# Preparing the first latent head's keys and queries ahead of four gate projections

## The chip, the cores and the metric

The kernel runs on one core of a Trainium2 chip. The metric is device time in microseconds (us) for one execution of the whole program. The core has a matrix engine (PE, with its weight loads PEld), a vector engine (DVE), an activation engine (ACT), a general engine (POOL) and the engine SP, whose queue issues nearly all the transfers of this kernel. Matrix results land in PSUM banks, from which ACT and DVE copy them to SBUF.

## The reference, cut to what matters

Two layers of a streaming encoder, for a prompt of 512 rows and a sample group of 64 rows with 1024 cached rows. Layer 0 runs latent attention (A) and stick-breaking attention (B) side by side; layer 1 runs two other attentions. Each layer ends in a gated output projection. What the change touches is attention A of the prompt group:

```
q_a, kv_a, k_r, g_a, ... = split_cols(h @ w_in, EVEN_SIZES)
c_kv   = rmsnorm(kv_a, kv_norm)            # latent, 128 wide
k_rope = apply_rope(k_r, pos)              # 32 wide
q      = einsum('bsc,chr->bshr', rmsnorm(q_a, q_norm), w_uq)   # 8 heads of 64 + 32
s      = (q . [w_uk c_kv ; k_rope]) * A_SCALE      # masked, then softmax per head
out_a  = (softmax(s) @ c_kv) @ w_uv
mixed  = [silu(g_a) * out_a ; silu(g_b) * out_b];  x += rmsnorm(mixed @ w_out)
```

The kernel builds the per-head keys (64 rows from `w_uk`, 32 rotary rows) and splits most operands in a high and a low part, so that most products are three matmuls.

## The kernel before, in words

The stretch in question is the passage from attention B to attention A in layer 0. In program order it reads:

1. `mla_queries(0)` (L968 on) projects the queries of heads 0 to 3, rotates them (`rope_q`) and leaves them in four tiles `qs`; `mla_vals(0)` makes the values of heads 0 to 3.
2. The last pair of heads of attention B, `sb_pair(3)`, with its sample part beside it, inside `tc.high_priority(PR_last)`.
3. Four gate projections, `gate_tile(a["ws"][12 + p], ...)`: each has two halves of weights (loaded, split by ACT into a high part `whi` at L166 and by POOL into a low part `wlo` at L170), two PSUM banks of 24 matmuls each (`ws_bank`, L253), and per bank one sigmoid on ACT (L624) and one product on DVE (L625).
4. The key tiles of head 0: `KH0`, `KL0` (high and low part) and the split of `w_uk` into `wukh`, `wukl` (L1016 to L1025); the rotary key rows are transposed on PE (L1023) and copied by ACT (L1024) and DVE (L1025).
5. Loads of `wuv` and `wukT` (L1027, L1028); the cached keys and values of the sample group (L1075 to L1106), most of them into the tile `arena`, which takes the room of `h0`'s first half and so waits for the last gate matmul that reads it.
6. `mix0`: four gated outputs of attention B are copied and split into the operand of the output projection (`mix`, high part on ACT L655, low part in turn on POOL and DVE, L656). It takes the room of `h0`'s second half.
7. `mla_prep(0)` (L932 on): three matmuls for head 0's keys (L939), evacuated by ACT (L940) and DVE (L941) into `KH0`, `KL0`; four transposes for its queries (L945), evacuated by ACT (L946) and DVE (L947) into two tiles `QH`, `QL`.
8. `mla_squeries(0)`, `mla_vals(1)` (L909 matmuls, L913 on ACT, L914 on DVE), and then the heads: `mla_head` prepares head h+1 and computes the scores of head h (L963, L964), whose first step on DVE is the row minimum L919.

What sets the order: the program runs in a planner that goes through the instructions, takes for each engine the one that comes first in program order among those that it holds ready by its own costs, and gives out the buffers as it goes; each engine then executes its list strictly in order. `high_priority` moves a block forward in that preference. So program order is a preference between instructions that are ready and no fixed place.

Buffers that the change touches: PSUM tag `psA` has two banks, shared by `gate_tile`, `mla_queries`, `mla_vals`, `mla_prep` and others; `psT` has two banks for transposes. The ring `R` has ten SBUF tiles: four for each pair of attention B, `wvh`, `wvl`, the four of step 4, `wuv`, `wukT`, and two per prepared head. `wraw` has four buffers for weights as loaded; `whi` and `wlo` have five each.

Of the kernel before, what the change touches and what calls it, by code (L numbers as in the profile page):

```python
# [26 lines left out]
NPAIR = H // 2  # L27
# [32 lines left out]
def f32(ap):  # L60
    return ap.bitcast(F32)
# [3 lines left out]
def kernel(ctx: ExitStack, tc: tile.TileContext, a: dict, o: dict):  # L65
# [11 lines left out]
    def nm(s):  # L77
        cnt[0] += 1
        return f"{s}_{cnt[0]}"
# [14 lines left out]
    def ring(shape, dt, tag, name=None):  # L94
        p, n = rings[tag]
        if isinstance(p, list):
            rings[tag][1] += 1
            return p[n % len(p)].tile(shape, dt, name=nm(name or tag), tag=tag, bufs=1)
        return p.tile(shape, dt, name=nm(name or tag), tag=tag, bufs=n)
# [4 lines left out]
    def Er(shape, name="e"):  # L104
        return ring(shape, F32, "E", name)

    def Rr(shape, name="r"):
        return ring(shape, F32R, "R", name)
# [49 lines left out]
    phase = [""]  # L158
# [80 lines left out]
    def ws_tiles(h, tiles, between=None):  # L239

        ws = [ws_weights(src, rooms) for src, _, rooms in tiles]
        for c0, c1 in CUTS:
            for (_, cb, _), w in zip(tiles, ws):
                ws_bank(w, h, cb, c0, c1)
            if between and c1 < TT:
                between()
# [56 lines left out]
    def drain():  # L303
        for _ in side[0]:
            pass
# [308 lines left out]
    def gate_tile(src, h, ft, raw):  # L614
        g = bp.tile([P, TT], F32, name=nm("g"), tag=f"g{ft}", bufs=1)
        gates[ft] = g

        def cb(ps, c0, c1):
            n = c1 - c0
            gv = g[:, c0:c1]  # L620
            th = Er([P, 320], "th")
            tv = th[:, :n]
            if raw:
                nc.scalar.activation(tv, ps[:, :n], AF.Sigmoid)  # L624
                nc.vector.tensor_mul(gv, ps[:, :n], tv)  # L625
            else:

                nc.scalar.activation(tv, ps[:, :n], AF.Tanh, scale=0.5)
                nc.vector.scalar_tensor_tensor(out=gv, in0=tv, scalar=1.0, in1=ps[:, :n], op0=ALU.add, op1=ALU.mult)

        ws_tiles(h, ((src, cb, ()),))
# [14 lines left out]
    def new_h(pool):  # L646
        f = new_feat(pool)
        for g in range(2):
            feat_half(f, g, g)
        return f  # L650
# [111 lines left out]
    h0 = new_h(big)  # L762
# [170 lines left out]
    def mla_prep(h):  # L933

        st = h % 2
        kp = psA()
        hs = slice(h * 64, (h + 1) * 64)
        for n, (w, c) in enumerate(((wukh, CTh), (wukh, CTl), (wukl, CTh))):
            nc.tensor.matmul(kp[:64], w[:, hs], c[:, 2, :S], start=(n == 0), stop=(n == 2))  # L939
        nc.scalar.copy(KH[st][:64], kp[:64])  # L940
        nc.vector.tensor_sub(KL[st][:64], kp[:64], f32(KH[st][:64]))  # L941
        QH, QL = Rr([P, S]), Rr([P, S])
        tp = psA()
        for t in range(NT):
            nc.tensor.transpose(tp[:96, t * P:(t + 1) * P], qt[h // 4][t][:, h % 4, :], ident)  # L945
        nc.scalar.copy(QH[:96], tp[:96])  # L946
        nc.vector.tensor_sub(QL[:96], tp[:96], f32(QH[:96]))  # L947
        return QH, QL
# [59 lines left out]
    with tc.high_priority(PR_last):  # L1008
        beside(sb_sample(3), EV_sb)
        sb_pair(3, pr)  # L1010
        drain()
    for p in range(NPAIR):
        gate_tile(a["ws"][12 + p], h0, p, True)

    phase[0] = ""
    KH0, KL0, wukh, wukl = (Rr([P, 512], x) for x in ("kh0", "kl0", "wukh", "wukl"))  # L1016
    wkr = w_tile("wraw", [P, 512], F32)
    nc.sync.dma_start(wkr, a["w_uk"])
# [4 lines left out]
        nc.tensor.transpose(tp[:32, t * P:(t + 1) * P], kr[:, t], ident)  # L1023
    nc.scalar.copy(KH0[64:96], tp[:32])  # L1024
    nc.vector.tensor_sub(KL0[64:96], tp[:32], f32(KH0[64:96]))  # L1025
    wuv, wukT = ring([P, 512], F32, "R", "wuv"), ring([P, NPAIR, P], F32, "R", "wukT")
    nc.sync.dma_start(wuv, a["w_uv"])  # L1027
    nc.sync.dma_start(wukT, a["w_ukT"])  # L1028
# [15 lines left out]
    def mla_squeries(hh):  # L1044

        qn = ring([P, 4, 64], F32, "sx", "qn")
        nc.gpsimd.tensor_copy(out=qn[:DS], in_=qf[:, 4 * hh:4 * hh + 4, :64])
        qnf = qn.rearrange("p h d -> p (h d)")
        t = psT()
        for p in range(2):  # L1050
            nc.tensor.transpose(t[:, p * DS:(p + 1) * DS], qnf[:DS, p * P:(p + 1) * P], ident[:DS, :DS])
        qnT = ring([P, P], F32, "sx", "qnT")
        nc.scalar.copy(qnT, t[:, :P])
        for s in range(2):
            t = psT()
            me = slice(64 * s, 64 * s + 64)
            for p in range(2):
                nc.tensor.matmul(t[:, p * DS:(p + 1) * DS], wukT[me, 2 * hh + p, :], qnT[me, p * DS:(p + 1) * DS],
                                 start=True, stop=True)
            tv = v3(t[:, :P])  # L1060
            qh, ql = (x[:, hh * 256:(hh + 1) * 256].rearrange("p (a s b) -> p a s b", a=2, s=2)[:, :, s, :]
                      for x in (QLh, QLl))
            nc.scalar.copy(qh, tv)
            nc.vector.tensor_sub(ql, tv, f32(qh))
        qh4 = qf[:, 4 * hh:4 * hh + 4, 64:96]
        qr3 = ring([P, 4, 96], F32R, "sx", "qr3")
        nc.scalar.copy(qr3[:DS, :, 0:32], qh4)
        nc.scalar.copy(qr3[:DS, :, 64:96], qh4)
        nc.vector.tensor_sub(qr3[:DS, :, 32:64], qh4, f32(qr3[:DS, :, 0:32]))
        t = psT()  # L1070
        for h in range(4):
            nc.tensor.transpose(t[:96, h * DS:(h + 1) * DS], f32(qr3)[:DS, h, :], ident[:DS, :DS])
        nc.scalar.copy(QR[:96, hh * 256:(hh + 1) * 256], t[:96, :256])
# [64 lines left out]
    for p in range(NPAIR):  # L1138
        mix(mix0, 1, p, gates[4 + p], eng=nc.vector if p % 2 else nc.gpsimd)
        mix_sample(mix0, 1, p, gates[4 + p])  # L1140
    QLh, QLl, KH1, KL1 = (bp.tile([P, 512], F32R, name=x, tag=f"g{i}", bufs=1)
                          for i, x in ((4, "qlh"), (5, "qll"), (6, "kh1"), (7, "kl1")))
    KH, KL = (KH0, KH1), (KL0, KL1)
    for x in (KH, KL):
        nc.gpsimd.tensor_copy(out=x[1][64:96], in_=f32(x[0][64:96]))
    part0 = dp.tile([TT, D], F32, name="part0")
    ready = {0: mla_prep(0)}
    mla_squeries(0)
    mla_vals(1)
    def mla_samples():  # L1150
# [365 lines left out]
def build(arrays):  # L1516
    import concourse.bacc as bacc

    nc = bacc.Bacc("TRN2", target_bir_lowering=False, num_devices=1)
    a, o = {}, {}  # L1520
    for name, v in arrays.items():
        a[name] = nc.dram_tensor(f"in_{name}_dram", v.shape, mybir.dt.from_np(v.dtype), kind="ExternalInput").ap()
    for i, (name, shape) in enumerate(_OUTS):
        ap = nc.dram_tensor(f"out_{i}_dram", shape, F32, kind="ExternalOutput").ap()
        rows = [d for d in shape if d != 1][0]
        n = int(np.prod(shape)) // rows
        o[name] = bass.AP(ap.tensor, 0, [[n, rows], [1, n]])
    with tile.TileContext(nc, schedule_with_timeline_sim=True) as tc:
        kernel(tc, a, o)
    return nc  # L1530
# [9 lines left out]
```

## Time and profile before

| what | value |
|---|---|
| median of 3 runs | 844.62 us (844.27 to 845.49) |
| profiled execution, its own time | 845.28 us |
| span in the trace, first to last instruction | 842.8 us |
| PE busy | 773.1 us (92% of the span) |
| DVE busy | 596.8 us (71%) |
| ACT busy | 451.0 us (54%) |
| POOL busy | 364.5 us (43%) |
| mean granted clock of PE | 0.978 of full speed |

The profiled execution takes 2.5 us more than its span and 0.66 us more than the median. A row of the timeline gives start, duration, engine, line, operation and operands, with the idle time of the engine before it and what ended that in brackets. All times of rows are us from the start of the span.

### The profile page before, as it was taken

To read this page: it belongs to the slowest core of one execution; us is meant where nothing else is said; L and a number is where in the kernel's file an instruction comes from. 1 tells how busy PE (TensorE), PEld (TensorE's weight loads), DVE (VectorE), ACT (ScalarE), POOL (GpSimd) and SP (SyncE) were. 2 spreads that over 40 slices of the span, in tenths; PEclk is the share of its full clock that TensorE was granted. 3 is DMA by queue.
4 is the path that set the end of the run, shared out by engine and by line. 5 is a ranking of instruction groups with operands and counts; after the bars stand their busy time and mean duration, and the time that the engine had idled before them with its cause. 6 is when DMAs were issued, how large, how long until landed. Compare 5 with 4: busy or idle time off the path is not lost.

```text
span 842.8 us, 16341 instructions
## 1 busy us (share of the span) xinstructions
PE 773.1 (92%) x5581; PEld 716.0 (85%) x5581; DVE 596.8 (71%) x1453; ACT 451.0 (54%) x1232; POOL 364.5 (43%) x464
## 2 busy tenths in 40 slices
PE   8889899999896999998889999999998999999996
PEld 6889798988795788796788989999997898998986
DVE  5566887797956767658984766686766777778655
ACT  7533563565755666554553545465434665658521
POOL 6574343554527012125673444353234343436343
PEclk9999999999998999998999999999999999999999
DMA  8143323622121111236353443334234442452472
GB/s 250 58 126 116 93 77 96 194 79 94 57 85 48 61 53 60 82 96 238 113 143 113 137 123 102 112 101 119 71 108 115 155 143 83 136 155 68 139 236 100
DMA packets 69924, 95.52 MB, mean 113 GB/s; under 512 B 9529, under 2 KB 40489, under 8 KB 69810
## 3 DMA queue, kind: packets, MB, share of 16 engines
q1 hardware_dynamic: 69264, 94.12, 36.8%
q8 instruction: 44, 0.72, 0.3%
q10 hardware_dynamic: 578, 0.37, 0.1%
q14 instruction: 38, 0.31, 0.1%
HBM read 74.36 MB, written 18.79 MB: 111 GB/s over the span
## 4 chain that ended last, share of the span: by engine, by line
PE 60%; DVE 16%; ACT 6%; issue 6%; DMA 5%; POOL 5%; SPq 1%; DVEq 0%; POOLq 0%; ACTq 0%
PE psA L253 21%; PE psA L263 15%; PE psU L427 4%; PE psX L516 4%; PE psT L418 3%; PE psA L271 3%; DVE r L361 2%; POOL wlo L170 2%; DVE whi L168 1%; PE psS L452 1%; DVE C L477 1%; PE psS L551 1%; DMA wraw<-in_w_out_dram 1%; PE psS L453 1%; ACT sx L570 1%
## 5 line engine op out<-in xcount | busy, mean ns | idle before, releaser
L253 PE MATMUL psA<-hT,whi 128*128 128x320 f32 (+1 forms) x1216 | 259.0, 301 | 5.4 <-DVE r L341 2.0
L170 POOL TENSOR_TENSOR wlo<-wraw,whi 128x512 fp32r<-128x512 f32 (+2 forms) x102 | 138.9, 1368 | 184.8 <-ACT whi L166 97.1
L253 PEld LDWEIGHTS psA<-hT,whi 128*128 128x128 f32 x1216 | 199.6, 191 | 8.8 <-DVE g L625 1.7
L253 PE MATMUL psA<-hT,wlo 128*128 128x320 f32 (+1 forms) x608 | 183.3, 302 | 0.0
L263 PE MATMUL psA<-whi,hT 128*128 128x256 f32 (+2 forms) x812 | 163.1, 288 | 8.3 <-DVE m L733 6.5
L263 PEld LDWEIGHTS psA<-whi,hT 128*128 128x128 f32 x812 | 130.2, 189 | 11.8 <-DVE m L733 7.7
L263 PE MATMUL psA<-wlo,hT 128*128 128x256 f32 (+2 forms) x420 | 121.4, 289 | 0.0
L253 PEld LDWEIGHTS psA<-hT,wlo 128*128 128x128 f32 x608 | 116.0, 191 | 0.3
L263 PEld LDWEIGHTS psA<-wlo,hT 128*128 128x128 f32 x420 | 80.1, 191 | 0.5
L166 ACT CAST whi<-wraw 128x512 fp32r<-128x512 f32 (+2 forms) x72 | 43.9, 614 | 33.7 <-PE psA L253 25.4
L168 DVE CAST whi<-wraw 128x512 fp32r<-128x512 f32 (+1 forms) x58 | 39.0, 674 | 18.9 <-PE psA L263 8.0
L363 POOL TENSOR_TENSOR kz<-kf,r 64x256 fp32r<-64x256 f32 x48 | 40.8, 851 | 23.3 <-DVE r L361 20.9
L477 DVE TENSOR_TENSOR_SCAN C<-C 128x384 f32<-128x384 f32 (+4 forms) x44 | 46.3, 1062 | 6.4 <-ACT C L475 6.1
L461 ACT ACTIVATE x<-x,st 128x128 f32<-128x128 f32 (+1 forms) x64 | 36.0, 562 | 22.2 <-DVE st L1227 21.7
L422 DVE TENSOR_TENSOR pt1l<-psT,pt1h 128x384 fp32r<-128x384 f32 x64 | 39.5, 619 | 10.2 <-ACT pt1h L421 9.1
L516 PE MATMUL psX<-vs,sP 128*128 128x256 f32 (+1 forms) x184 | 40.5, 315 | 6.4 <-DVE vs L543 5.6
L529 POOL TENSOR_TENSOR sK<-kraw,sK 128x384 fp32r<-128x384 f32 (+2 forms) x32 | 32.5, 1016 | 30.4 <-ACT sK L528 24.6
L421 ACT CAST pt1h<-psT 128x384 fp32r<-128x384 f32 x64 | 34.0, 533 | 21.7 <-PE psT L418 20.2
L439 POOL TENSOR_TENSOR g<-g,oT 128x512 f32<-128x512 f32 x14 | 18.9, 1347 | 56.5 <-DVE oT L431 56.4
L452 PE MATMUL psS<-r,r 128*128 128x256 f32 (+1 forms) x96 | 34.6, 362 | 6.7 <-DVE st L1227 6.2
L1227 DVE CUSTOM_DVE_ANT_0 x<-psS,T 128x128 f32<-128x128 f32 (+1 forms) x64 | 30.8, 481 | 11.4 <-PE psT L418 10.1
L431 DVE SCALAR_TENSOR_TENSOR oT<-psU,oT 64x256 f32<-64x256 f32 x64 | 26.8, 419 | 16.9 <-ACT oT L430 15.9
(391 smaller groups left out, 1953.0 us busy)
## 6 DMA issues: line engine op xcount, KB each, us to landing
wraw<-in_ws_dram SPq DMA_DIRECT2D x80, 256.0 KB, 2.8
wraw<-in_w_out_dram SPq DMA_DIRECT2D x32, 256.0 KB, 2.8
x<-in_x_prompt_dram SPq DMA_DIRECT2D x16, 256.0 KB, 5.2
part<-part SPq DMA_DIRECT2D x32, 128.0 KB, 2.1
m<-part SPq DMA_DIRECT2D x16, 256.0 KB, 5.6
r<-r SPq DMA_DIRECT2D x48, 64.0 KB, 2.0
out_dram<-kout SPq DMA_DIRECT2D x12, 256.0 KB, 2.7
out_dram<-vf SPq DMA_DIRECT2D x24, 128.0 KB, 1.8
```

Source lines behind the costliest of these rows:

```text
L166: nc.scalar.copy(hi, raw)
L168: nc.vector.tensor_copy(out=hi, in_=raw)
L170: eng.tensor_sub(lo, raw, f32(hi))
L253: nc.tensor.matmul(ps[:, :c1 - c0], w[:, k % 4, :], h.m[k // 4][:, k % 4, x, c0:c1], start=(k == 0 and n == 0), stop=(k == KT - 1 and n == 2))
L263: nc.tensor.matmul(ps[:, :n], h.m[k // 4][:, k % 4, x, t * P:(t + 1) * P], w[:, k % kp, :], start=(k == ks[0] and m == 0), stop=(k == ks[- ...
L363: nc.gpsimd.tensor_sub(pair.kl[s][me, cs], kf[me, cs], f32(k[me, cs]))
L421: nc.scalar.copy(ph[:, :i + 1, at], tv)
L422: nc.vector.tensor_sub(pl[:, :i + 1, at], tv, f32(ph[:, :i + 1, at]))
L452: nc.tensor.matmul(ps[:, :w], pair.qq[s][:, q], pair.kk[s][:, :w], start=True, stop=False)
L461: nc.scalar.activation(w[:, :n], src, AF.Exp, bias=mn, scale=-1.0, accum_out=sm)
L477: nc.vector.tensor_tensor_scan(out=c[:, :n][:, ::-1], data0=c[:, :n][:, ::-1], data1=c[:, :n][:, ::-1], initial=1.0 if carry is None else ...
L516: nc.tensor.matmul(po[:, :256], l, r, start=(first and n == 0), stop=(last and n == len(ops) - 1))
```

## The change

`mla_prep(0)` and the key tiles it needs (steps 4 and 7) are put ahead of the four gate projections (step 3). The pair lists `KH`, `KL` are made early with only their first entry; the second, `KH1`, `KL1`, is filled in where it was made before. The three matmuls, four transposes, their four copies, the load and split of `w_uk`, and the rotary key rows all stay the same instructions; the loads of `wuv` and `wukT` stay behind the gates. The assignment `phase[0] = ""` (which engines split weights) stays behind the gates as well.

```
         sb_pair(3, pr)
         drain()
-    for p in range(NPAIR):
-        gate_tile(a["ws"][12 + p], h0, p, True)
-
-    phase[0] = ""
+
     KH0, KL0, wukh, wukl = (Rr([P, 512], x) for x in ("kh0", "kl0", "wukh", "wukl"))
     wkr = w_tile("wraw", [P, 512], F32)
     nc.sync.dma_start(wkr, a["w_uk"])
...
     nc.vector.tensor_sub(KL0[64:96], tp[:32], f32(KH0[64:96]))
+    KH, KL = [KH0, None], [KL0, None]
+    ready = {0: mla_prep(0)}
+    for p in range(NPAIR):
+        gate_tile(a["ws"][12 + p], h0, p, True)
+
+    phase[0] = ""
     wuv, wukT = ring([P, 512], F32, "R", "wuv"), ring([P, NPAIR, P], F32, "R", "wukT")
...
-    KH, KL = (KH0, KH1), (KL0, KL1)
+    KH[1], KL[1] = KH1, KL1
     for x in (KH, KL):
         nc.gpsimd.tensor_copy(out=x[1][64:96], in_=f32(x[0][64:96]))
     part0 = dp.tile([TT, D], F32, name="part0")
-    ready = {0: mla_prep(0)}
     mla_squeries(0)
     mla_vals(1)
```

## Rows read from the trace of the kernel before

**Rows 1.** Busy time by stretch: length, PE, PEld, DVE, ACT, POOL, PE clock, DMA.
```profile
219.50:228.50 9.00, 6.21 (x43) 4.68 (x41) 8.97 (x17) 7.37 (x20) 7.20 (x9) 1.00 0.23 81
228.50:260.40 31.90, 31.90 (x243) 31.05 (x242) 17.44 (x35) 16.06 (x38) 7.83 (x12) 1.00 0.20 63
260.40:270.30 9.90, 2.79 (x19) 1.52 (x17) 8.20 (x8) 5.16 (x14) 9.76 (x9) 0.79 0.33 93
270.30:276.40 6.10, 6.08 (x25) 5.40 (x26) 4.75 (x12) 3.90 (x9) 3.97 (x4) 0.51 0.46 136
276.40:400.00 123.60, 115.59 (x800) 100.30 (x799) 85.95 (x250) 74.21 (x211) 28.68 (x34) 0.97 0.30 94
...
```
**Rows 2.** What PE waited for from 260 to 345 us: total, times, longest.
```profile
PE psA L909 <- DVE kl L941: 5.2, 1, 5.2
PE psS L963 <- ACT r L946: 1.4, 1, 1.4
...
```
**Rows 3.** Timeline of PE, 256 to 275 us, six of its rows.
```profile
256.00 0.60 PE L1023 MATMUL psT<-ident,kr 128*32 128x128 f32 x4
...
260.61 0.66 PE L1058 MATMUL psT<-qnT,wukT 64*128 64x64 f32 x8
261.73 0.44 PE L939 MATMUL psA<-cth,wukh 128*64 128x512 f32 x1 [0.46 <-ACT ks L1089]
...
262.24 0.39 PE L939 MATMUL psA<-cth,wukl 128*64 128x512 f32 x1
262.71 0.64 PE L945 MATMUL psA<-ident,qs 128*96 128x128 f32 x4
...
274.28 0.63 PE L909 MATMUL psA<-r,cth 128*128 128x256 f32 x2
```
**Rows 4.** Timeline of DVE, 264 to 274 us, six of its rows.
```profile
264.82 3.45 DVE L656 TENSOR_TENSOR hT<-g,hT 128x512 fp32r<-128x512 f32 x2
268.19 1.48 DVE L168 CAST whi<-wraw 128x512 fp32r<-128x512 f32 x1
269.60 0.67 DVE L941 TENSOR_TENSOR kl<-psA,kh 64x512 fp32r<-64x512 f32 x1
270.20 0.67 DVE L947 TENSOR_TENSOR r<-psA,r 96x512 fp32r<-96x512 f32 x1
270.79 1.50 DVE L170 TENSOR_TENSOR wlo<-wraw,whi 128x512 fp32r<-128x512 f32 x1
...
272.95 0.27 DVE L919 TENSOR_REDUCE st<-psS 128x1 f32<-128x128 f32 x1
...
```
**Rows 5.** Timeline of ACT, 261 to 265 us, one row.
```profile
263.65 0.58 ACT L940 CAST kh<-psA 64x512 fp32r<-64x512 f32 x1
...
```
**Rows 6.** All L168 copies of the kernel: duration in ns, least, median, most.
```profile
L168 DVE CAST whi<-wraw x58: 390/428/1549, 40.0 to 806.6; 128x512 fp32r<-128x512 f32 x56, 128x528 fp32r<-128x528 f32 x2
```
**Rows 7.** Busy time by stretch, columns as in rows 1, one stretch of 2 us.
```profile
266.00:268.00 2.00, 0.00 (x0) 0.00 (x0) 2.00 (x2) 0.79 (x3) 2.00 (x3) 0.52 0.23 83
...
```
**Rows 8.** Timeline of PE, DVE and POOL around the first gate matmul, one fence.
```profile
227.85 1.33 POOL L1020 TENSOR_TENSOR wukl<-wraw,wukh 128x512 fp32r<-128x512 f32 x1 [0.73 <-ACT wukh L1019]
228.02 0.39 DVE L914 TENSOR_TENSOR v<-psA,v 128x256 fp32r<-128x256 f32 x1
228.46 0.51 PE L253 MATMUL psA<-hT,whi 128*128 128x256 f32 x2
229.97 0.41 DVE L914 TENSOR_TENSOR v<-psA,v 128x256 fp32r<-128x256 f32 x1
233.42 0.39 DVE L625 TENSOR_TENSOR g<-psA,th 128x256 f32<-128x256 f32 x1
...
```
**Rows 9.** Timeline of SP and POOL, loads and the last step of `sb_pair(3)`.
```profile
224.57 0.33 SPq L1018 DMA_DIRECT2D wraw<-in_w_uk_dram  x1
249.79 0.43 SPq L1028 DMA_DIRECT2D wukT<-in_w_ukT_dram  x1
254.11 1.29 POOL L439 TENSOR_TENSOR g<-g,oT 128x512 f32<-128x512 f32 x1 [9.02 <-DVE oT L431]
```

## The prediction

> **What bounds the kernel now.** The page comes first: PE is busy for 92% of the span, so time is lost where PE stands still or runs slowly. The busy table by stretch around the moved step shows where [rows 1]. From 219.5 to 228.5 us DVE is full (8.97 of 9.00 us) and PE stands still for 9.00 - 6.21 = 2.8 us. From 228.5 to 260.4 PE is full: that is the four gate projections with the rest of `sb_pair(3)` between them. From 260.4 to 270.3 PE works 2.79 of 9.90 us while POOL is full (9.76) and DVE nearly (8.20). From 270.3 to 276.4 PE is full again, but its granted clock is 0.51. From there to 400 us PE is busy for 115.59 of 123.60 us.
>
> The list of waits names the hole: 5.2 us of PE, once, for DVE's L941, and 1.4 us for ACT's L946 [rows 2]. Both are evacuations of `mla_prep(0)`. In PE's timeline its seven matrix instructions (three L939, four L945) stand at 261.7 to 263.4, right behind the gates, and the third of the four L909 groups of `mla_vals(1)` starts only at 274.28 [rows 3]. ACT makes its key copy at 263.65, at once [rows 5]. DVE comes to the matching L941 at 269.60, because two subtractions of `mix0` (L656, 3.45 us) and a weight copy (L168) stand ahead of it in its list; L947 follows, then a weight subtraction (L170), and the first softmax step of head 0, L919, starts at 272.95 [rows 4]. Both banks of `psA` are held until L941 and L947 are done, so `mla_vals(1)` can't start either: that is why the wait is booked on L909.
>
> **What goes (the gain).** With head 0 prepared before the gates end, both `psA` banks are free for `mla_vals(1)` once the last gate bank is evacuated. The gates end at 260.4; PE then has two groups of L909 and the first scores of head 0 to do while DVE works off `mix0`. What is late next is the evacuation of these values: DVE still can't leave `mix0` before 264.82 + 3.45 = 268.27. Two L914 of 0.4 us [rows 8] follow, and L919 starts at 268.27 + 0.8 = 269.07 instead of 272.95: 3.9 us earlier. The bounds: if DVE's list keeps its weight work where it is, only L941 and L947 drop out of it, 270.79 - 269.60 = 1.2 us. If PE sets the pace, the third group of L909 starts after one L914, at 268.67 instead of 274.28: 5.6 us. I take 3.9, since head 0's own chain runs through L919. The 1.48 and 1.50 us of L168 and L170 are pushed back; the weights are for the output projection and DVE has room in 270.3 to 276.4 (4.75 of 6.10 us) and after (85.95 of 123.60). Since PE is 94% busy behind, a start moved forward is carried to the end of the stage.
>
> A rule speaks for the lower bound. In this stretch L168 takes 1.48 us where its median over 58 copies is 428 ns [rows 4, 6], with POOL full beside it [rows 1]. L941 and L947, which read PSUM, take 0.67 us there. The Trainium skill (SBUF — State Buffer, section "SBUF: two separate sides") says that DVE and POOL share one pair of SBUF ports as an exclusive lock, so that one of them stands still for the other's whole instruction. By it the two engines' SBUF work is one queue, and the change takes nothing out of that queue; the sum would then have 1.2 us in place of 3.9. The trace agrees on the slow copy; whether DVE's list is rearranged behind `mix0` it can't say.
>
> **What is added ahead of the gates (the price).** The step lands where DVE and PE are full.
> - PE: three L939 start 0.25 us apart ((262.24 - 261.73) / 2), the four L945 0.12 us apart (0.64 less one tail, over three), together 1.2 us that lay in the hole for nothing and now lie in or before the full stretch. The four L1023 transposes ran in the full stretch already, at 256.00 [rows 3]: no change.
> - `psA`: the last two groups of `mla_vals(0)` give their banks back at 228.41 and 230.38, when their L914 end; gate 12 takes the first at 228.46 [rows 8]. In program order the prep now comes before it. L939 0.7 us, ACT's copy 0.58, DVE's subtraction 0.67: the bank is free again at about 230.4, so gate 12 starts some 1.9 us later, the 1.2 us of PE within it. From below it is nothing: the prep fits the 2.8 us in which PE stands still before 228.5. From above: DVE's unbroken list runs to the first gate's L625 at 233.42 + 0.39 = 233.8; served last, the prep would hold both banks until then, 5.3 us. I take 1.9, the two copies served in turn.
> - DVE and ACT: L1025, L941, L947 (2.0 us on DVE), L1024, L940, L946 on ACT, ahead of `sb_pair(3)`'s end. That block's last step ends on POOL at 255.4 [rows 9], and `mix0` starts with the gates' end at 260.4: 5 us cover it; a delay beyond that moves `mix0` by the whole rest. Queued behind a waiting L941 or L947 on DVE are the scans of `sb_pair(3)`, which wait that long too.
> - The load of `w_uk` (issued at 224.57, last behind the gates' weights) goes ahead of eight gate loads in SP's order and takes one of four `wraw` buffers; its subtraction on POOL (1.33 us, ended 229.2) goes ahead of the gates' own [rows 8, 9]. All gate loads had been issued by 224.57, the first gate matmul is at 228.46, and POOL has 1.8 us free in that stretch: nothing. Without that cover it is the 1.33 us.
> - `QH`, `QL` take two tiles of the ring `R` ahead of `wuv` and `wukT`. `wukT` was issued at 249.79 and is read at 260.61: nothing, with some 8 us in hand.
>
> **Sum.** 3.9 - 1.9 = 2.0 us faster. On the profiled execution: 845.28 (span 842.8 and 2.5 around it) - 2.0 = 843.3 us. The median of the runs is 0.66 us lower: 842.6.
>
> **Rivals.**
> 1. *The wait only changes its owner.* PE fills its first two banks, then waits for L914 in place of L941, behind the same DVE list: gain 1.2, price 1.2 to 1.9, so 844.6 to 845.3. The same time comes out if the planner leaves the prep late: program order is a preference, and L1023 shows that an instruction can slip far into another's stretch. For: POOL full beside DVE. Against: L914 and L919 come ahead of the output weights in program order; but so did L941, and one L168 stood ahead of it all the same, so this weighs little.
> 2. *The banks are held before the gates* (the other side). Both `psA` banks wait with the prep for a DVE that has sb scans to do until 233.8; gate 12 starts 5.3 us late, and the whole full stretch moves back. With a gain of 3.9 that is +1.4, with 1.2 it is +4.1: 846.0 to 848.7, middle 847.4. It decides as soon as the price passes the gain. For: DVE 8.97 of 9.00 busy there, and only two banks. Against: the v groups before it got their banks back within two microseconds of each other, at 228.41 and 230.38, from the same full DVE.
> 3. *The clock stays up.* The clock fell to 0.52 (the lower level, 1.2 GHz) in 266 to 268, when PE had done next to nothing since the last L945 ended at 263.35 [rows 1, 3, 7], and 6.1 us of full work ran at 0.51. If PE's added work in the hole keeps it at 2.4 GHz, half of that, 3.0 us, comes on top: 839.6. Against: some 4 us of waiting remain before 268.3.
>
> **How the numbers follow.** Forecast 0.42 (842.6; own range 839.0, gain 5.6 with no price, to 843.7, gain 3.9 with a price of 3.0), rival 1 0.27, rival 2 0.23, rival 3 0.08. The other stages keep their instructions, but the planner lays the rest out anew, which may move a microsecond either way. What one can tell from no change here is about 0.2%, 1.7 us: faster means below 842.9. Faster: most of the forecast (0.36), rival 3, a little of rival 1: 0.46. Slower, above 846.3: most of rival 2 and a little beside it: 0.24. Same: 0.30. The range, 839.2 to 847.6, goes from rival 3 to the middle of rival 2.
>
> **What will show it.** Right: L939 and L945 for head 0 before the first matmul of gate 12, no PE wait for L941 near 265, L909 directly behind the last gate, L919 about 8.5 us after the gates' end (now 12.5), the gates' end within 2 us of 260.4. Wrong: a PE wait for L914 of 4 us or more with L919 still 11 us or more behind the gates' end (rival 1); a gap of several us before gate 12 with PE waiting for L941 or L947 there (rival 2); clock at 1.00 in the stretch after the gates (rival 3).

## The result, and the profile after

The change makes the kernel slower: 859.24 us (median of 4 runs, 856.15 to 861.63) against 844.44 us before (4 runs, 844.18 to 845.49). The comparison gives a ratio of 1.0142, 95% interval 1.0115 to 1.0170; the two medians alone would give 1.0175. The profiled execution took 858.36 us, its span is 856.2 us: 13.4 us more than before (842.8). The moved lines are numbered three lower than before (L1018, L1023 and L1025 are L1015, L1020 and L1022 here), those behind them two or three higher.

The busy table by stretch answers to [rows 1]. A stretch has come in that before had not:

```profile
230.60:243.90 13.30, 10.38 (x50) 7.29 (x49) 11.01 (x25) 7.25 (x20) 0.76 (x4) 0.78 0.12 40
243.90:272.50 28.60, 28.60 (x215) 27.95 (x214) 7.39 (x16) 12.81 (x25) 6.64 (x7) 0.98 0.16 45
272.50:282.00 9.50, 1.48 (x8) 0.94 (x7) 7.90 (x8) 4.50 (x13) 9.41 (x8) 0.66 0.36 97
282.00:288.50 6.50, 6.02 (x28) 4.78 (x29) 4.26 (x11) 3.19 (x8) 3.93 (x4) 0.71 0.49 161
```

From 230.6 to 243.9 PE works off `sb_pair(3)` alone, with gaps, and its granted clock falls to 0.78 (1.00 in the same place before [rows 1]). PE's timeline there, to be held against [rows 3, 8]:

```profile
230.62 0.44 PE L939 MATMUL psA<-cth,wukh 128*64 128x512 f32 x1
...
232.29 0.61 PE L945 MATMUL psA<-ident,qs 128*96 128x128 f32 x4 [0.64 <-DVE v L914]
...
241.81 1.05 PE L418 MATMUL psT<-ident,w 128*128 128x128 f32 x4
242.66 1.06 PE L1020 MATMUL psT<-ident,kr 128*32 128x128 f32 x4
...
243.92 0.64 PE L253 MATMUL psA<-hT,whi 128*128 128x256 f32 x2
```

The preparation's matrix work comes where the program has it, and takes both `psA` banks. The first matmul (L253) of gate 12, the first of the four gates, follows 13.3 us after L939; before it came at 228.46 [rows 8]. ACT's timeline and DVE's show what the banks waited for:

```profile
232.32 0.57 ACT L940 CAST kh<-psA 64x512 fp32r<-64x512 f32 x1
...
243.76 0.57 ACT L1021 CAST kh<-psT 32x512 fp32r<-32x512 f32 x1 [0.27 <-PE psT L1020]
244.35 0.58 ACT L946 CAST r<-psA 96x512 fp32r<-96x512 f32 x1
```
```profile
242.46 0.43 DVE L431 SCALAR_TENSOR_TENSOR oT<-psU,oT 64x256 f32<-64x256 f32 x1 [0.68 <-ACT oT L430]
242.92 0.68 DVE L941 TENSOR_TENSOR kl<-psA,kh 64x512 fp32r<-64x512 f32 x1
...
244.36 0.68 DVE L1022 TENSOR_TENSOR kl<-psT,kh 32x512 fp32r<-32x512 f32 x1
245.07 0.69 DVE L947 TENSOR_TENSOR r<-psA,r 96x512 fp32r<-96x512 f32 x1
```

L941 could have run when L940 ended, at 232.9. It has no wait in brackets at 242.92: it stands ten microseconds down DVE's list, behind the evacuations of `sb_pair(3)` and beside the rotary rows (L1020 to L1022). It does not wait for those either: it starts before ACT writes them (L1021 at 243.76). That the two stand together is the planner's list, and why it lists them so is not shown.

Behind the gates DVE and PE read (compare [rows 4] and the wait in [rows 2]):

```profile
262.76 0.29 DVE L919 TENSOR_REDUCE st<-psS 128x1 f32<-128x128 f32 x1
...
275.46 1.30 DVE L168 CAST whi<-wraw 128x512 fp32r<-128x512 f32 x1 [0.95 <-DMA wraw<-in_w_out_dram]
276.68 3.43 DVE L656 TENSOR_TENSOR hT<-g,hT 128x512 fp32r<-128x512 f32 x2
280.03 1.48 DVE L168 CAST whi<-wraw 128x512 fp32r<-128x512 f32 x1
281.43 0.74 DVE L914 TENSOR_TENSOR v<-psA,v 128x256 fp32r<-128x256 f32 x2
```
```profile
272.14 0.31 PE L253 MATMUL psA<-hT,wlo 128*128 128x320 f32 x1
...
281.90 0.80 PE L909 MATMUL psA<-r,cth 128*128 128x256 f32 x2 [6.72 <-DVE v L914]
...
286.05 0.39 PE L939 MATMUL psA<-cth,wukh 128*64 128x512 f32 x1
```
L253 here is the gates' last matmul, and L939 the next head's preparation. The same two of the kernel before:
```profile
260.27 0.31 PE L253 MATMUL psA<-hT,wlo 128*128 128x320 f32 x1
...
276.90 0.39 PE L939 MATMUL psA<-cth,wukh 128*64 128x512 f32 x1
```

The list in front of the waiting evacuation is the one of before, weight copy included; PE now waits 6.7 us for L914 in place of 5.2 for L941. Head 0's first softmax step, L919, ran before the gates' end (262.76) and is no longer in it.

**Where the 13.4 us arise.** Every DVE instruction before was paired with the same one in the other trace; the table gives the median lag in a stretch of 15 us, and in the last columns its growth from one to the next. "At 765" is the stretch at 690 for runs 9 and 10, whose order differs behind it, so that their last two columns don't compare with the others.

```
                        lag (us) at                     growth
                     165    210    300    765    825    load   step   middle  end
changed kernel      0.10   2.16   9.46  10.01  13.34   +2.1   +7.3   +0.6   +3.3
1 rotary only      -1.39  -0.95  -2.08   1.19   1.17   +0.4   -1.1   +3.3    0.0
2 prep, rotary      2.15   2.71   5.00   6.18   9.38   +0.6   +2.3   +1.2   +3.2
3 psX               2.72   3.55   3.01   6.32   7.20   +0.8   -0.5   +3.3   +0.9
4 after 3 gates     0.75   0.76   3.91   4.31   8.25    0.0   +3.2   +0.4   +3.9
5 rotary in psX    -0.38   0.20   4.34   6.57   6.65   +0.6   +4.1   +2.2   +0.1
6 values moved      4.15   4.75  11.51  10.55  10.04   +0.6   +6.8   -1.0   -0.5
7 casts on ACT      1.22   0.10  -3.75  -3.44  -3.06   -1.1   -3.9   +0.3   +0.4
8 psX, casts        0.00   2.08  -0.77   2.60   2.55   +2.1   -2.9   +3.4    0.0
9 before, order C   0.97  -0.18  -1.15   1.27   1.29   -1.2   -1.0   +2.4    0.0
10 after, order C   2.25   3.00   8.90  12.41  12.18   +0.8   +5.9   +3.5   -0.2
11 behind gates    -0.19  -1.31   1.08   1.58   5.13   -1.1   +2.4   +0.5   +3.6
12 same, casts      0.44  -0.71  -1.81   1.06   1.13   -1.2   -1.1   +2.9   +0.1
13 load only        2.13   4.23   4.49   5.16   4.66   +2.1   +0.3   +0.7   -0.5
14 run 8, POOL     -0.92  -0.95  -4.43  -3.07  -3.18    0.0   -3.5   +1.4   -0.1
```

One trace each: the first column and "middle" differ between traces by up to 5.5 us with no order in it, and are left unexplained. "Step" and "end" fall into groups, and so does the load once it is read close by (run 13). Runs 9 and 10 are the two kernels of the case once more, up to 740 us: their steps are -1.0 and 5.9 where those of the case are 0 and 7.3, so a step read from one trace is good to some 1.5 us. Three places, then: 7.3 us at the step, 3.3 at the end of the kernel, 2.1 before the step.

### The profile page after: what moved, and what is told of

It is laid out like the page before. It is cut to its first block, busy times and chain, and to the rows that moved or that the text cites. A ratio compares the mean times of both kernels' runs of the same rounds, so it can differ in the third digit from the quotient of the medians.

```text
span 856.2 us, 16349 instructions
## 1 busy us (share of the span) xinstructions
PE 777.1 (91%) x5581; PEld 719.0 (84%) x5581; DVE 595.9 (70%) x1453; ACT 453.9 (53%) x1234; POOL 363.9 (43%) x464
## 4 chain that ended last, share of the span: by engine, by line
PE 59%; DVE 17%; ACT 8%; issue 6%; DMA 5%; POOL 4%; SPq 1%; DVEq 0%; POOLq 0%; ACTq 0%
PE psA L253 20%; PE psA L263 16%; PE psU L427 4%; PE psX L516 3%; PE psT L418 3%; PE psA L271 2%; DVE r L361 2%; DVE C L477 1%; DMA wraw<-in_w_out_dram 1%; DMA kraw<-in_fox_kT_dram 1%; ACT sx L570 1%; PE psS L452 1%; DVE whi L168 1%; PE psS L551 1%; PE psS L453 1%
## 5 line engine op out<-in xcount | busy, mean ns | idle before, releaser
L253 PE MATMUL psA<-hT,whi 128*128 128x320 f32 (+1 forms) x1216 | 257.8, 301 | 5.9 <-DVE r L341 2.5
L253 PEld LDWEIGHTS psA<-hT,whi 128*128 128x128 f32 x1216 | 199.4, 191 | 9.2 <-issue 3.0
L253 PE MATMUL psA<-hT,wlo 128*128 128x320 f32 (+1 forms) x608 | 182.8, 301 | 0.0
L253 PEld LDWEIGHTS psA<-hT,wlo 128*128 128x128 f32 x608 | 115.7, 190 | 0.3
L168 DVE CAST whi<-wraw 128x512 fp32r<-128x512 f32 (+1 forms) x58 | 38.3, 661 | 15.4 <-PE psA L253 6.0
L421 ACT CAST pt1h<-psT 128x384 fp32r<-128x384 f32 x64 | 33.9, 533 | 21.0 <-PE psT L418 19.4
L516 PEld LDWEIGHTS psX<-vs,sP 128*128 128x128 f32 (+1 forms) x184 | 28.3, 195 | 11.9 <-DVE vs L543 4.4
```

What stands on the lines that cost most here:

```text
L168: nc.vector.tensor_copy(out=hi, in_=raw)
L253: nc.tensor.matmul(ps[:, :c1 - c0], w[:, k % 4, :], h.m[k // 4][:, k % 4, x, c0:c1], start=(k == 0 and n == 0), stop=(k == KT - 1 and n == 2))
L516: nc.tensor.matmul(po[:, :256], l, r, start=(first and n == 0), stop=(last and n == len(ops) - 1))
```

## Experiments

Diffs are against the kernel after the change, unless said otherwise. "Before" is the unchanged kernel on the same chip in the same rounds. The letters A to H are theories; each stands in the expectation that tests it first. "Late" is a start against the kernel before, less the lag that the trace has at 210 us already.

**Run 1. Rotary only.** `mla_prep(0)` back behind the gates; load, split and rotary rows stay ahead.
```
-    ready = {0: mla_prep(0)}
     for p in range(NPAIR):
         gate_tile(a["ws"][12 + p], h0, p, True)
...
+    ready = {0: mla_prep(0)}
     mla_squeries(0)
```


> Only the w_uk load and split and the rotary key rows (L1015 to L1022) stay ahead of the four gates; the first head's preparation goes back behind them. Theory A (the preparation holds both psA banks, because DVE's KL copy L941 comes only behind the rotary rows, which come only behind the score blocks of the last softmax-back pair): the gates start as before, near 228.5 to 231 us, and the time is 842 to 847. Theory B (the copies lose to the pair's work by priority): the same, 842 to 847, since no bank is held. Theory C (what costs is the moved load, split and rotary rows themselves, or the later loads that they displace): the time stays over 852.

846.91 us, before 846.60; ratio 1.0013 (0.9989 to 1.0038). Gate 12 starts at 227.52, which is not late at all (the trace is 0.95 us ahead). The cost at the step is the preparation's; C falls as its main cause.

**Run 2. Preparation, then rotary rows.**
```
+    KH, KL = [KH0, None], [KL0, None]
+    ready = {0: mla_prep(0)}
     tp = psT()
...
     nc.vector.tensor_sub(KL0[64:96], tp[:32], f32(KH0[64:96]))
-    KH, KL = [KH0, None], [KL0, None]
-    ready = {0: mla_prep(0)}
```


> The same work as in the changed kernel, all of it ahead of the gates; only the order within it is turned: the first head's preparation (KH and KL rows 0 to 63, QH, QL) stands ahead of the rotary rows 64 to 95. Theory A: L941 reads KH0, of which L1021 is a writer when it stands earlier in the program; turned round it has nothing to wait for but L940, so L941 runs within 4 us of L940 (at 233 to 237 instead of 242.92), the first gate-12 matmul at 232 to 236 instead of 243.92, and the time is 844 to 851. Theory B: nothing is gained by the order, L941 stays at 242 to 244 behind the pair's copies, gate 12 starts at 243 to 245, the time is 856 to 861. Theory C: also 856 to 861.

852.49 us, before 846.60; ratio 1.0068 (1.0039 to 1.0096), 1.5 us over what A allowed. The trace bears A out:
```profile
235.74 0.65 DVE L941 TENSOR_TENSOR kl<-psA,kh 64x512 fp32r<-64x512 f32 x1
237.46 0.65 DVE L947 TENSOR_TENSOR r<-psA,r 96x512 fp32r<-96x512 f32 x1
```
```profile
236.45 0.50 PE L253 MATMUL psA<-hT,whi 128*128 128x256 f32 x2
```
L941 now follows L940 (232.87) by 2.9 us instead of 10.6, and gate 12 is 5.3 us late (236.45 against 228.46 + 2.71) instead of 13.3. That is the upper end of the price in the prediction. The order of two pieces of one tile decided where L941 stood. B predicted no change.

**Run 3. The preparation's sums in `psX`.**
```
-        kp = psA()
+        kp = psX()
...
-        tp = psA()
+        tp = psX()
```
(for head 0 alone)

> The first head's preparation writes its two PSUM groups in the psX bank instead of psA; the order of the program is that of the changed kernel. Theory A and theory B: the two psA banks stay with the gates, gate 12 starts at 228 to 231 us, the gates end near 262, and what is lost is at most the turns of psX that the sample's sums (L516) wait for: 842 to 848. Theory C: 854 to 861.

847.46 us, before 846.60; ratio 1.0011 (0.9987 to 1.0035). Gate 12 starts at 232.01, the gates end at 265.77, both in a trace that is 3.55 us late at 210 already. So gate 12 is not late, and the gates end 1.6 us late (1.6 too in runs 8 and 14, which use the same bank). With the gates' banks left alone the price is 1.6 us in place of 9.7. The next head's L939 comes 13.7 us behind the gates' end (279.51), 2.6 less than before, and what is left of the gain is the half microsecond in the table.

**Run 4. Behind three gates.**
```
+    for p in range(3):
+        gate_tile(a["ws"][12 + p], h0, p, True)
     KH0, KL0, wukh, wukl = ...
...
-    for p in range(NPAIR):
+    for p in range(3, NPAIR):
         gate_tile(a["ws"][12 + p], h0, p, True)
```


> Load, split, rotary rows and preparation stand behind three of the four gates and ahead of the last. By then the last softmax-back pair is done (its last PV sum ends near 253 us), so under theory A the rotary rows follow at once, the banks are given back in about 2 us, and the lead of the preparation over the gates' end stays: 841 to 846. Theory B: with the pair's copies done, nothing outranks the preparation's: 841 to 846 too. Theory C: 850 or more. A fourth possibility, that the wait of the value projection's third group (L909 on DVE's L914, 6.7 us in the changed kernel) eats the lead: 844 to 846 with such a wait of 5 us or more behind the gates.

853.35 us, before 846.60; ratio 1.0071 (1.0039 to 1.0103): of the four expectations only C's is met, and not for C's reason. PE's waits from 215 to 345 us say why:
```profile
PE psA L909 <- DVE v L914: 4.1, 1, 4.1
PE psT L418 <- DVE sP L503: 3.7, 1, 3.7
```
The second is at 221 to 225, before the moved lines: with the preparation elsewhere the planner had also listed the evacuations of attention B and its sample part another way (before, this wait was 0.6 us). By 225 to 240 the lag has grown by 2.8 of its 3.2 us. The first is the hole behind the gates. C's condition, that the moved load costs, does not hold here (no growth at the load). The run does not test what the move behind three gates is worth by itself.

**Run 5. Rotary rows in `psX`.** One word: `tp = psT()` becomes `tp = psX()`.

> The changed kernel with one word changed: the rotary rows' four transposes (L1020) write a psX bank instead of a psT bank. Theory A, now in this form: L941 stands behind L1021 because both touch KH0, and L1020 stands behind the transposes of the last pair because it wants a psT bank. Then L1020 moves from 242.66 to 234 to 239 (it now waits for the sample's sums in psX only), L941 comes within 2 us behind it, the first gate-12 matmul at 236 to 241, and the time is 850 to 856. If the wait for psT is not the link (the copies lose to the pair's work), L941 and gate 12 stay at 242 to 245 and the time at 856 to 861. The written order of the last score blocks near the end (from about 775 us), which in the changed kernel and in runs 2 and 4 was another one than in the kernel before, is here that of the kernel before; if that order costs 2 to 3 us, the distance to the kernel before grows by less than 1.5 us between 765 and 810, where it grew by 3.3 in the changed kernel.

853.90 us, before 847.75; ratio 1.0072 (1.0039 to 1.0104). The trace, DVE and PE:
```profile
235.88 0.68 DVE L941 TENSOR_TENSOR kl<-psA,kh 64x512 fp32r<-64x512 f32 x1
237.53 0.68 DVE L1022 TENSOR_TENSOR kl<-psX,kh 32x512 fp32r<-32x512 f32 x1
239.06 0.68 DVE L947 TENSOR_TENSOR r<-psA,r 96x512 fp32r<-96x512 f32 x1
```
```profile
236.12 0.60 PE L1020 MATMUL psX<-ident,kr 128*32 128x128 f32 x4
236.94 0.48 PE L253 MATMUL psA<-hT,whi 128*128 128x256 f32 x2
```
L1020 moves from 242.66 to 236.12, and L941 and gate 12 with it; gate 12 is 8.3 us late (236.94 against 228.46 + 0.20) instead of 13.3. So 5.0 us of the delay hang on one bank: `psT`, wanted by the rotary transposes, is in use by `sb_pair(3)`; the rotary rows come late; L941, listed with them, comes late; `psA` stays held. The other 8.3 us this run leaves; the order of run 2 takes 8.0 of the 13.3 away, and the bank of run 3 all of it. The end has the old order, and there the lag grows by 0.1.

**Run 6. Values before the last gate**, on the kernel of run 2.
```
-    for p in range(NPAIR):
+    for p in range(3):
         gate_tile(a["ws"][12 + p], h0, p, True)
+    mla_vals(1)
+    gate_tile(a["ws"][15], h0, 3, True)
```


> The kernel of run 2 (preparation, then rotary rows, ahead of the gates) with the second half of the value projection (mla_vals(1)) put between the third and the last gate. Theory D (the wait of L909 for DVE's L914 behind the gates, 6.7 us in the changed kernel and 5.2 us for L941 before, costs the lead): L909 waits under 1 us anywhere, head 0's first exponentials follow the gates at once, the second head's preparation starts 11 to 13 us behind the gates' end instead of 14.2, and the time is 2 to 4 us under run 2: 846 to 850. Theory E (what sets the distance is DVE's and POOL's own list behind the gates: four differences L656, the casts L168 and L170, which need the gates' end; TensorE's work moved ahead only makes the hole emptier and the gates later): the second head's preparation stays 13.5 us or more behind the gates' end, the gates end 1 to 1.5 us later than in run 2, no gain from it. The order of the last blocks near the end is that of the kernel before, as in run 5: if it is worth 2 to 3 us, those 2 to 3 us are gained there under either theory.

855.61 us, before 847.75; ratio 1.0106 (1.0066 to 1.0146). D is wrong. Of E, that nothing is gained came true, its numbers did not: the gates end 4.8 us later than in run 2 (274.46 against 267.64 + 2.04) where it had 1 to 1.5, and the next head's L939 comes at 275.60, 1.1 us behind the gates' end where it had 13.5 or more. But its evacuation waits. PE's longest wait, and DVE's list:
```profile
PE psA L963 <- DVE r L947: 7.9, 2, 7.0
```
```profile
282.06 1.48 DVE L168 CAST whi<-wraw 128x512 fp32r<-128x512 f32 x1
283.46 0.68 DVE L947 TENSOR_TENSOR r<-psA,r 96x512 fp32r<-96x512 f32 x1
```
The owner changes a third time, to the next head's L947. Counted from the gates' end, the evacuation that PE waits for starts at 269.60 - 260.58 = 9.0 us before, 281.43 - 272.45 = 9.0 after the change and 283.46 - 274.46 = 9.0 here. What stands first in `psA` makes no difference; DVE's list does. In runs 1, 4, 5 and 11 that list begins with an L656 in place of the L168, and the same distance is 7.8 us; without the casts it is 5.0 (runs 7 and 12) or 6.2 (8 and 14).

**Run 7. Casts on ACT**, on the kernel before. `phase[0] = ""`, which hands half of the output weights' casts to DVE, is set after the first output column instead of behind the gates.
```
-    phase[0] = ""
...
         out_first(0, mix0, 1, part0, "part", OF[p])
+        phase[0] = ""
```


> The kernel before, with one assignment moved: the weight casts of the first output column behind the gates (two L168, one L170: 4.4 us of DVE at 263.5 to 272.2 in the kernel before) go to ScalarE and GpSimd; the preparation stays behind the gates. Theory E: DVE's list behind the gates sets when head 0's softmax and the second head start; without the casts L941 runs 2.5 to 3 us earlier (266.5 to 267.5), the second head's preparation starts 13 to 15 us behind the gates' end instead of 16.5, and the time falls by 1.5 to 3.5 us: 841 to 843.5 where the kernel before gives 844.5. If GpSimd's list takes its place (it is 99% busy from 260 to 270): no change, 844 to 846.

842.66 us, before 847.75; ratio 0.9946 (0.9924 to 0.9969): faster than both kernels of the case, the lowest ratio of all runs.
```profile
262.85 2.85 DVE L656 TENSOR_TENSOR hT<-g,hT 128x512 fp32r<-128x512 f32 x2
265.63 0.67 DVE L941 TENSOR_TENSOR kl<-psA,kh 64x512 fp32r<-64x512 f32 x1
```
```profile
266.36 0.80 PE L909 MATMUL psA<-r,cth 128*128 128x256 f32 x2 [2.92 <-DVE kl L941]
```
L941 starts 5.0 us behind the gates' end (260.68) instead of 9.0, and PE's wait for it falls from 5.2 [rows 2] to 2.9.

**Run 8. `psX` and casts on ACT**: runs 3 and 7 together.

> Run 3 (the preparation ahead of the gates, its sums in psX) with the casts of run 7 taken off VectorE. Theory E: the gain of run 7 comes on top of run 3, that is 1.5 to 3.5 us under run 3's 847.5: 844 to 846. If both shorten the same hole they don't add: 846 to 848.

844.86 us, before 847.75; ratio 0.9980 (0.9959 to 1.0001). As expected, and with its median still 2.2 us above run 7's, though the two intervals overlap. The traces show why the move adds nothing even in `psX`: the next head's L939 comes 11.0 us behind the gates' end in place of 12.6 in run 7, and the gates end 1.6 us late. The lag at the load (+2.1) comes on top.

**Runs 9 and 10. One order at the end.** In the kernel before (run 9) and in the changed one (run 10): `PR_fox = 200` becomes `PR_fox = 210`.

> The kernel before with one number changed, the priority of the last attention's score blocks (PR_fox, 200 to 210). It leaves the order of everything up to about 740 us as it was and gives the last stretch a third order, which is the same one in this run and in the next. By itself it tells only what that order costs: 843 to 851. It is the partner of run 10.

> The changed kernel with the same number changed, so that both have one order near the end. Theory F (of the 13 to 15 us that the change costs, 7.3 arise at the moved step and 3.3 near the end, where the score blocks and the output's first half are written in another order): the distance from run 9 to run 10 is 6.5 to 9.5 us, where it was 14.8 between the kernels of the case, and in the traces the distance does not grow by more than 1 us after 765 us. Theory G (the late loss follows from the step itself, by the clock or by transfers that arrive in another rhythm, and not from the written order): the distance from run 9 to run 10 stays at 12 to 15 us and still grows by 3 us near the end.

849.88 and 857.24 us, before 846.88; ratios 1.0030 (1.0011 to 1.0049) and 1.0108 (1.0081 to 1.0136). The distance between the two is 7.4 us, 14.8 between the kernels of the case; the new order by itself costs the kernel before 3.0 us by the medians. Between their traces it is 3.2 us at 210, 10.1 at 300, 11.1 at 690 and 10.9 at 825: nothing is added at the end. F holds. The four traces with PE's order of the changed kernel there (it, runs 2, 4 and 11) lose 3.2 to 3.9 us at the end, the nine with PE's order of before 0.9 at most. The loss is PE's: in the busy table of the kernel before, and of the changed one at the same work,
```profile
765.00:785.00 20.00, 17.81 (x134) 15.77 (x134) 16.83 (x50) 15.28 (x46) 8.82 (x9) 1.00 0.25 77
...
800.00:815.00 15.00, 14.23 (x116) 13.68 (x115) 8.39 (x18) 4.90 (x13) 7.45 (x7) 1.00 0.87 278
```
```profile
775.00:795.00 20.00, 16.47 (x121) 14.15 (x121) 15.51 (x48) 14.70 (x45) 8.01 (x9) 1.00 0.16 50
...
813.40:828.40 15.00, 13.25 (x99) 13.07 (x98) 6.98 (x14) 3.47 (x9) 6.33 (x7) 0.89 0.78 276
```
PE stands still for longer, and the clock dips. What in the moved lines made the planner choose another order 500 us later is open.

**Runs 11 and 12. Half the way.** The preparation goes behind the gates but ahead of `mix0`; run 12 has it ahead of the rotary rows and the casts of run 7 on ACT.
```
     for p in range(NPAIR):
         gate_tile(a["ws"][12 + p], h0, p, True)
     KH0, KL0, wukh, wukl = ...
...
+    ready = {0: mla_prep(0)}
...
     part0 = dp.tile([TT, D], F32, name="part0")
-    ready = {0: mla_prep(0)}
```
(against the kernel before)

> The preparation is moved half the way: ahead of the mixing of the first four gates (mix0, L655 and L656) and the weight casts, but behind the four gates; load, split and rotary rows stay behind the gates. Theory E (the list of VectorE and ScalarE behind the gates sets the lead, and the move past the gates is what costs): gate 12 starts as before, the preparation's copies come ahead of L656, L941 at 263 to 267 instead of 269.6, the second head's preparation 14 to 16 us behind the gates' end instead of 16.3. The written order near the end is here the one of the changed kernel, and by theory F costs 3.3 us: the time is 845 to 849, near or above the kernel before. If theory F is wrong: 841 to 844.

> The half move of run 11 (with the preparation ahead of the rotary rows, as in run 2) and the casts off VectorE of run 7; the order near the end is that of the kernel before. Theory E and F: the best of all, 840 to 843, equal to run 7 or up to 2 us under it. If the preparation's copies are late behind the gates for another reason than the list (the bank, or KH0), it stays at 844 or more.

853.83 and 847.49 us, before 846.88; ratios 1.0083 (1.0054 to 1.0113) and 1.0006 (0.9987 to 1.0025). Both missed, run 11 by 5 us and run 12 by 4.5. In neither did the copies come ahead of `mix0`: in run 11 both L656 and both L168 still stand before L941 (267.05), and the next head's L939 (277.02) comes 17.8 us behind the gates' end in place of 16.3. In run 12 the first evacuation does come at 5.0 us behind the gates, and yet it gains 2.8 us less at the step than run 7. The busy table of run 7, then of run 12:
```profile
268.00:272.00 4.00, 4.00 (x19) 3.54 (x18) 2.34 (x8) 3.13 (x8) 3.86 (x5) 0.50 0.16 41
272.00:276.00 4.00, 4.00 (x25) 3.37 (x23) 3.12 (x9) 1.70 (x4) 2.98 (x4) 0.89 0.70 199
```
```profile
268.00:272.00 4.00, 4.00 (x19) 2.95 (x18) 1.98 (x8) 3.12 (x8) 3.97 (x4) 0.50 0.26 75
272.00:276.00 4.00, 4.00 (x16) 3.12 (x15) 2.04 (x4) 1.17 (x3) 2.46 (x3) 0.50 0.66 201
```
Run 12 keeps the lower clock some 4 us longer, in full work; that is an estimate of 4 us x (0.89 - 0.50), some 1.6 us. The preparation holds one bank from 259.7 on and both from 262.0, so the sample's key transposes want the bank behind L941 (265.57, with a wait of 2.92 us) and its query products start at 269.14; in run 7 both are done in the first microsecond behind the gates, at 260.61 and 260.70. E was too narrow: DVE's list sets when the first evacuation comes, but in this trace what PE is left with in the hole, and its clock, count as well; no run separates these two.

**Run 13. The load alone**, on the kernel before: the `w_uk` load, `wukh` and `wukl` move from behind the gates to ahead of them, nothing else.
```
+    KH0, KL0, wukh, wukl = ...
+    wkr = w_tile("wraw", [P, 512], F32)
+    nc.sync.dma_start(wkr, a["w_uk"])
+    nc.scalar.copy(wukh, wkr)
+    nc.gpsimd.tensor_sub(wukl, wkr, f32(wukh))
     for p in range(NPAIR):
         gate_tile(a["ws"][12 + p], h0, p, True)
...
-    KH0, KL0, wukh, wukl = ...
-    wkr = w_tile("wraw", [P, 512], F32)
-    nc.sync.dma_start(wkr, a["w_uk"])
-    nc.scalar.copy(wukh, wkr)
-    nc.gpsimd.tensor_sub(wukl, wkr, f32(wukh))
```


> The kernel before with the w_uk load and its split alone (three lines) moved ahead of the four gates; rotary rows, preparation and all else as before. Theory H (the cast of w_uk stands in ScalarE's list ahead of the copies of the score block then running, and waits for its transfer with the copies behind it): ScalarE waits 5 us or more for w_uk near 180 to 186, TensorE's wait for pt0h behind it is about 2.4 us instead of 1.5 for pt0l, the trace is 1.1 to 1.6 us behind at 187, and the time is 0.5 to 2 us over the kernel before. If the load costs nothing, as the prediction had it: within 0.5 us of the kernel before, and no such wait.

848.42 us, before 847.40; ratio 1.0010 (0.9992 to 1.0027). Its time alone can't be told from no change; its trace can. SP of the changed kernel, then ACT and PE of run 13:
```profile
183.25 0.38 SPq L1015 DMA_DIRECT2D wraw<-in_w_uk_dram  x1
```
```profile
188.46 0.62 ACT L1016 CAST wukh<-wraw 128x512 fp32r<-128x512 f32 x1 [6.03 <-DMA wraw<-in_w_uk_dram]
```
```profile
189.40 0.58 PE L427 MATMUL psU<-pt0h,v 128*128 128x256 f32 x1 [2.47 <-ACT pt0h L421]
```
The load is issued 41 us earlier than before (224.57 [rows 9]), and ACT's list has its cast ahead of an L421 that a running score block needs. At the products next to it (187.47 before) the lag has grown by 1.1 to 1.6 us in all nine traces with the cast there on ACT, and by nothing or less in the others. In the changed kernel it is 1.5 of the 2.1 us; the rest is no more than other traces drift between 165 and 210 us without it (-1.2 to 0.0 in the table).

**Run 14. Run 8 with that cast on POOL.**
```
-    nc.scalar.copy(wukh, wkr)
+    nc.gpsimd.tensor_copy(out=wukh, in_=wkr)
```


> Run 8 (preparation ahead of the gates in psX, output casts off VectorE) with the high part of w_uk cast by GpSimd instead of ScalarE. Theory H: ScalarE no longer waits for the transfer, the trace is level with the kernel before at 187 (within 0.4 us), the rest is as in run 8, and the time is 1 to 2 us under run 8's 0.998 of the kernel before, that is 0.995 to 0.997. If it was not ScalarE's wait but the transfer itself (its place ahead of the weight loads in SyncE's list), the 1.1 to 1.6 us stay at 187 and the ratio at 0.998.

845.49 us, before 847.40; ratio 0.9975 (0.9955 to 0.9995).
```profile
185.51 0.39 PE L427 MATMUL psU<-pt0l,v 128*128 128x256 f32 x1 [1.44 <-DVE pt0l L422]
```
PE waits 1.44 us for DVE, as before, and the lag does not grow; the load is still issued ahead of the gates' own. So, in the trace, it was ACT's wait and not the transfer. Of the expected 1 to 2 us the ratio shows 0.4, inside its interval, so the time does not bear it out. It has the lowest ratio of the versions that keep the change; run 7, without it, has a lower one, with overlapping intervals.

## Why the prediction was wrong

Forecast 842.6 us, measured 859.24; the sign was wrong.

- **What bounds the kernel** was read rightly: the hole behind the gates, the two banks, DVE's list. Run 7 shows it, 4 us of that list removed and some 4.6 us gained (0.54%).
- **The price is the step that failed**: "I take 1.9, the two copies served in turn", with 5.3 as its upper end. Gate 12 started 13.3 us late (243.92 against 228.46 + 2.16), the gates ended 9.7 us late (272.45 against 260.58 + 2.16; their stretch is 28.6 us long in place of 31.9, since `sb_pair(3)` no longer runs between them). Rival 2 had the mechanism and the place, with DVE's list ending at 233.8; and run 2, without the rotary rows in front, comes to its 5.3 us. What it lacked is that L941 was listed with L1021 and L1022, and that these hang on a third bank, `psT`, in use by `sb_pair(3)` (run 5). Of the term itself 1.6 us is what runs 3, 8 and 14 leave when the bank is not held. "The four L1023 transposes ran in the full stretch already: no change" was the row to stop at: before, they ran at 256.00 [rows 3], 27 us later than where the preparation was to be done.
- **The gain** was to be 3.9 us, with L914 right behind `mix0`. The second L168 stayed ahead of it (280.03), and PE waited 6.72 us for L914: rival 1's wait. The reason given for 3.9, "since head 0's own chain runs through L919", failed too: L919 came at 262.76, 9.7 us before the gates' end, and PE's hole behind the gates stayed, now until the values' L914. The next head's L939 came 13.6 us behind the gates' end (272.45) instead of 16.3 (260.58), a gain of 2.7; in runs 9 and 10, the same two kernels to here, 13.5 and 15.3, so 1.8. 9.7 - 2.7 = 7.0, near the 7.3 of the table. The Trainium skill (SBUF — State Buffer, "SBUF: two separate sides") was weighed for an unmoved list, as one queue of DVE and POOL. The list was indeed unmoved. Whether the two engines are one queue there, no run tells: of the three pieces that run 7 takes from DVE two go to ACT, and the third runs on POOL only behind L941, at 268.81.
- **The `w_uk` load, costed at nothing**, was 1.5 us in the trace, of 2.1 before the step. The cover named was on SP and POOL; the ACT cast was not looked at, and that the load would move by 41 us, not past the gates alone, was not foreseen.
- **The end of the kernel** had no term, only "may move a microsecond either way". It was 3.3 us.
- 2.1 + 7.3 + 0.6 + 3.3 = 13.3 of the 13.4 us of span. The sum has to come out, since the columns are differences of one lag; it proves no cause. That is done by the runs: 1, 2, 3 and 5 for the step, 9 and 10 for the end, and for the load 13 and 14, in their traces alone.
- **Rival 3** did not come: behind the gates the clock was 0.66 in the hole (0.79 before) and 0.71 in the stretch after it (0.51 before), not 1.00. It fell where the prediction had no term for it: 0.50 from 238 to 244 us, with PE busy for 5.7 of the 6 us, in the new stretch. By an estimate from these two numbers half of that work, 2.9 us, is part of the price.

## What to carry to other kernels

Before work is moved past a full stretch, follow every bank and tile that its evacuations touch back to whoever holds it, one link further than the first, and check the in-order list of each engine that gets an instruction, casts of a moved load included. A hole that ends with an evacuation belongs to the list of the evacuating engine: taking foreign work out of that list (run 7) paid where moving the waiting work (the change, runs 3 and 6) did not. Where a planner writes the order, pin the far stages to one order before comparing two versions.

## What was not expected of the hardware

After a hole PE stayed at the lower clock, 1.2 GHz, in full work: in run 12 the granted clock was 0.50 from 268 to 276 us with PE busy 4.00 of 4.00 us in both rows shown above; in run 7, whose hole held 2.93 us of PE's work from 260 to 264 against 1.21, it was up again 4 us earlier. The rows of that stretch, run 7 and then run 12:
```profile
260.00:264.00 4.00, 2.93 (x21) 1.75 (x19) 2.51 (x4) 4.00 (x11) 4.00 (x4) 1.00 0.39 101
```
```profile
260.00:264.00 4.00, 1.21 (x7) 0.47 (x5) 3.42 (x4) 3.95 (x9) 4.00 (x4) 0.87 0.55 133
```
That the fuller hole is the reason is not shown. The same DVE copy (128x512) that took 1.30 and 1.48 us beside a full POOL behind the gates has a median of 428 ns [rows 6].
